# A row softmax on one core: five of eight tile loads move from Sync's queue to ScalarE's, ahead of the stores

## Chip, cores and metric

The kernel runs on one core of one Trainium2 chip. The metric is device time in microseconds (us) of one execution. It reads 33.55 MB from HBM and writes as much, so both the moving of data and the work on it matter.

## What is computed

A softmax over the last axis of a 16 x 1024 x 512 array of float32, with the input divided by a temperature of 0.5:

```python
def reference(x):
    temp = 0.5
    x_scaled = x / temp
    x_max = np.max(x_scaled, axis=-1, keepdims=True)
    exp_x = np.exp(x_scaled - x_max)
    return (exp_x / np.sum(exp_x, axis=-1, keepdims=True)).astype(np.float32)
```

## The kernel before

The 16,384 rows of 512 numbers are cut into eight tiles (`C = 8`, called chunks in the code). A tile holds 128 partitions with 16 rows each: 128 x 16 x 512 float32, 4.19 MB, 32 KB in each partition. There are six buffers (`BUFS`, L42), so tiles 6 and 7 reuse those of tiles 0 and 1. The order of the instructions is written out by hand (`manual_schedule`, L47): each engine and each queue works through its own instructions in program order, and the framework puts in the waits that the data needs.

Tile 0 is loaded in two pieces of 4 and 12 rows, all others whole (`LOADS`, L38). The work is done in 11 blocks (`BLOCKS`, L39): three for tile 0 (4, 4 and 8 rows), one for each of tiles 1 to 6, two of 8 rows for tile 7. Each tile is stored whole (`STORES`, L40), after its last block.

For a block, these steps follow one another:

- `load` (L59): the load of the block's tile, issued on Sync's queue (L66), if the tile has not been asked for yet. For tiles 6 and 7 the load has to wait until the store of tile 0 or 1 has landed, since it overwrites that buffer.
- `shift` (L68): VectorE takes the negated maximum of each row (L74) and doubles it (L78).
- `exponentials` (L80): ScalarE computes exp(2x - 2max) row by row, with the row's sum as a second result (L85).
- `scale_vector` (L95): VectorE takes the reciprocal of the sums (L100) and multiplies seven eighths of the rows (L102). `scale_scalar` (L106) leaves the last eighth to ScalarE (L111).
- `store` (L115): if the block ends its tile, ScalarE issues the tile's store on its own queue (L119).

The loop at the end (L123 to L133) staggers them: the exponentials of block i + 1 come before the scaling of block i, and the maximum of block i + 2 after it. On VectorE the order is thus scale i, maximum i + 2, scale i + 1, and so on.

Two hardware queues for transfers are in use. Sync's holds all loads: nine transfers, of which seven (tile 0's two pieces and tiles 1 to 5) are issued one after another at the start, as nothing holds them. ScalarE's holds the eight stores, from the moment that each tile is finished. Both queues are served by the same 16 transfer engines.

Before the first block, ScalarE loads its table of the exponential and runs it once on a dummy, `warm` (L50 to L52), so that the table is there when the first tile is.

Of the kernel before, what the change touches and what calls it, by code (L numbers as in the profile page):

```python
# [1 line left out]

# [4 lines left out]


@with_exitstack
def kernel(  # L10
    ctx: ExitStack,
    tc: tile.TileContext,
    x: bass.AP,
    out: bass.AP,
):
    nc = tc.nc
    fp32 = mybir.dt.float32
    P = nc.NUM_PARTITIONS
    AX = mybir.AxisListType.X
    EXP = mybir.ActivationFunctionType.Exp  # L20
    COPY = mybir.ActivationFunctionType.Copy
    MAX = mybir.AluOpType.max

    D = x.shape[-1]
    xf = x.flatten_outer_dims()
    of = out.flatten_outer_dims()
    N = xf.shape[0]

    G = 16
    C = N // (P * G)
    assert C * P * G == N
    xr = xf.rearrange("(c p g) d -> c p g d", p=P, g=G)
    outr = of.rearrange("(c p g) d -> c p g d", p=P, g=G)
    WHOLE = [(0, G)]
    LOADS = [[(0, 4), (4, G)]] + [WHOLE] * 7  # L38
    BLOCKS = [[(0, 4), (4, 8), (8, G)]] + [WHOLE] * 6 + [[(0, 8), (8, G)]]  # L39
    STORES = [WHOLE] * 8  # L40
    BMAX = 16
    BUFS = 6  # L42

    data = ctx.enter_context(tc.tile_pool(name="data", bufs=BUFS))
    stats = ctx.enter_context(tc.tile_pool(name="stats", bufs=6))

    ctx.enter_context(tc.manual_schedule())  # L47


    warm = stats.tile([P, 1], fp32, name="warm", bufs=1)  # L50
    nc.vector.memset(warm, 0.0)  # L51
    nc.scalar.activation(out=warm, in_=warm, func=EXP)  # L52

    chunks = {}
    blocks = [(c, lo, hi) for c in range(C) for lo, hi in BLOCKS[c]]
    n = len(blocks)
    biases, sums, recips = {}, {}, {}

    def load(c):  # L59
        if c < BUFS:  # L60
            chunks[c] = data.tile([P, G, D], fp32, name="xt")
        else:
            chunks[c] = chunks[c - BUFS]
        xt = chunks[c]
        for lo, hi in LOADS[c]:
            nc.sync.dma_start(out=xt[:, lo:hi, :], in_=xr[c][:, lo:hi, :])  # L66

    def shift(i):  # L68
        c, lo, hi = blocks[i]
        if c not in chunks:  # L70
            load(c)
        b = hi - lo
        negmax = stats.tile([P, BMAX], fp32, name="negmax")
        nc.vector.tensor_reduce(  # L74
            negmax[:, 0:b], chunks[c][:, lo:hi, :], axis=AX, op=MAX, negate=True
        )
        biases[i] = stats.tile([P, BMAX], fp32, name="bias")
        nc.vector.tensor_scalar_mul(biases[i][:, 0:b], negmax[:, 0:b], 2.0)  # L78

    def exponentials(i):  # L80
        c, lo, hi = blocks[i]
        sums[i] = stats.tile([P, BMAX], fp32, name="sums")
        for g in range(hi - lo):
            row = chunks[c][:, lo + g, :]
            nc.scalar.activation(  # L85
                out=row,
                in_=row,
                func=EXP,
                bias=biases[i][:, g : g + 1],
                scale=2.0,  # L90
                accum_out=sums[i][:, g : g + 1],
            )


    def scale_vector(i):  # L95
        c, lo, hi = blocks[i]
        b = hi - lo
        k = b - b // 8
        recips[i] = stats.tile([P, BMAX], fp32, name="recip")
        nc.vector.reciprocal(recips[i][:, 0:b], sums[i][:, 0:b])  # L100
        rows = chunks[c][:, lo : lo + k, :]
        nc.vector.tensor_mul(  # L102
            rows, rows, recips[i][:, 0:k].unsqueeze(2).broadcast_to((P, k, D))
        )

    def scale_scalar(i):  # L106
        c, lo, hi = blocks[i]
        b = hi - lo
        for g in range(b - b // 8, b):
            row = chunks[c][:, lo + g, :]  # L110
            nc.scalar.activation(  # L111
                out=row, in_=row, func=COPY, scale=recips[i][:, g : g + 1]
            )

    def store(i):  # L115
        c, _, end = blocks[i]
        for lo, hi in STORES[c]:
            if hi == end:
                nc.scalar.dma_start(  # L119
                    out=outr[c][:, lo:hi, :], in_=chunks[c][:, lo:hi, :]  # L120
                )

    shift(0)  # L123
    shift(1)
    exponentials(0)
    for i in range(n):
        if i + 1 < n:
            exponentials(i + 1)
        scale_vector(i)
        scale_scalar(i)  # L130
        if i + 2 < n:
            shift(i + 2)
        store(i)  # L133


# [1 line left out]
_INS = ['x']  # L137
_OUTS = [((16, 1024, 512), 'float32')]


# [23 lines left out]
```

## Time and profile before

| | us |
|---|---|
| median of 6 runs | 162.36 (162.09 to 162.48) |
| profiled execution, its time | 162.26 |
| profiled execution, its span | 160.5 |
| VectorE (DVE) busy | 134.6 (84%) |
| ScalarE (ACT) busy | 102.1 (64%) |
| VectorE idle, waiting for loads | 9.6 |
| first store issued | 45.67 |
| last store issued | 147.64 |

The span runs from the first to the last instruction that the profiler saw; the rest of the execution's time, 1.76 us, lies around it. In the lines of the profile, L66 is line 66 of the kernel, DVE is VectorE, ACT is ScalarE, SP is Sync, and ACTq and SPq are the parts of ScalarE and Sync that issue transfers. A group's row gives its line, engine and operation, output and input, shapes and count, then the busy time, the mean in ns of one, and the idle time before it with what ended it. These are the largest groups:

```profile
L85 ACT ACTIVATE xt<-xt,bias 128x512 f32<-128x512 f32 x128 | 90.4, 708 | 41.8 <-DVE bias L78 41.3
...
L102 DVE TENSOR_TENSOR xt<-xt,recip 128x7168 f32<-128x7168 f32 (+2 forms) x11 | 62.0, 5637 | 0.4
```

The section on transfers counts the issues and gives the size of each in KB and the median time from issue to landing:

```profile
out_dram<-xt ACTq DMA_DIRECT2D x8, 4096.0 KB, 22.8
xt<-in_x_dram SPq DMA_DIRECT2D x7, 4096.0 KB, 30.3
xt<-in_x_dram SPq DMA_DIRECT2D x1, 3072.0 KB, 11.8
xt<-in_x_dram SPq DMA_DIRECT2D x1, 1024.0 KB, 5.0
```

The single transfers, as the trace has them:

| transfer | issued at | us to landing |
|---|---|---|
| tile 0, first piece | 0.73 | 5.0 |
| tile 0, second piece | 1.15 | 11.8 |
| tile 1, 2, 3 | 1.63, 2.09, 2.80 | 21.0, 30.3, 39.5 |
| tile 4, 5 | 3.29, 3.78 | 52.9, 71.7 |
| tile 6, 7 | 69.64, 89.00 | 25.3, 26.0 |
| store 0, 1 | 45.67, 59.12 | 23.9, 29.8 |
| store 2, 3 | 75.74, 92.36 | 32.6, 28.6 |
| store 4, 5 | 108.98, 125.59 | 21.7, 14.7 |
| store 6, 7 | 133.17, 147.64 | 16.8, 12.0 |

### The profile page before, as it was taken

To read this page: it belongs to the slowest core of one execution; us is meant where nothing else is said; L and a number is where in the kernel's file an instruction comes from. 1 tells how busy PE (TensorE), PEld (TensorE's weight loads), DVE (VectorE), ACT (ScalarE), POOL (GpSimd) and SP (SyncE) were. 2 spreads that over 40 slices of the span, in tenths; PEclk is the share of its full clock that TensorE was granted. 3 is DMA by queue.
4 is the path that set the end of the run, shared out by engine and by line. 5 is a ranking of instruction groups with operands and counts; after the bars stand their busy time and mean duration, and the time that the engine had idled before them with its cause. 6 is when DMAs were issued, how large, how long until landed. Compare 5 with 4: busy or idle time off the path is not lost.

```text
span 160.5 us, 402 instructions
## 1 busy us (share of the span) xinstructions
DVE 134.6 (84%) x45; ACT 102.1 (64%) x273; POOL 0.2 (0%) x4
## 2 busy tenths in 40 slices
DVE  0507999999999999999999999999999999957000
ACT  3071549069979972998199909991899891690000
POOL 0000000000000000000000000000000000000000
DMA  5999999999999999999999999999999999999993
GB/s 180 468 431 482 400 400 490 417 392 459 449 400 376 408 408 490 408 400 498 408 392 498 417 392 484 417 400 466 441 400 433 474 400 417 490 400 400 498 408 139
DMA packets 2450, 67.13 MB, mean 418 GB/s; under 512 B 272, under 2 KB 272, under 8 KB 272
## 3 DMA queue, kind: packets, MB, share of 16 engines
q1 hardware_dynamic: 1296, 33.56, 49.3%
q10 hardware_dynamic: 1152, 33.55, 48.4%
q14 instruction: 2, 0.02, 0.0%
HBM read 33.55 MB, written 33.55 MB: 418 GB/s over the span
## 4 chain that ended last, share of the span: by engine, by line
DVE 80%; DMA 7%; ACT 4%; issue 0%; SPq 0%
DVE negmax L74 42%; DVE xt L102 36%; DMA xt<-in_x_dram 7%; ACT xt L85 4%; DVE bias L78 1%; DVE recip L100 1%; SPq L66 0%
## 5 line engine op out<-in xcount | busy, mean ns | idle before, releaser
L85 ACT ACTIVATE xt<-xt,bias 128x512 f32<-128x512 f32 x128 | 90.4, 708 | 41.8 <-DVE bias L78 41.3
L74 DVE TENSOR_REDUCE negmax<-xt 128x16 f32<-128x8192 f32 (+2 forms) x11 | 69.9, 6352 | 9.6 <-DMA xt<-in_x_dram 9.6
L102 DVE TENSOR_TENSOR xt<-xt,recip 128x7168 f32<-128x7168 f32 (+2 forms) x11 | 62.0, 5637 | 0.4
L85 ACT ACTIVATION_READ_ACCUMULATOR xt<-xt,bias 128x1 f32 x128 | 23.9, 187 | 0.0
L111 ACT ACTIVATE xt<-xt,recip 128x512 f32<-128x512 f32 x15 | 9.9, 707 | 0.0
L100 DVE RECIPROCAL recip<-sums 128x16 f32<-128x16 f32 (+2 forms) x11 | 2.4, 218 | 1.8 <-ACT xt L85 1.8
L78 DVE TENSOR_SCALAR bias<-negmax 128x16 f32<-128x16 f32 (+2 forms) x11 | 1.9, 173 | 0.4
L52 ACT ACT_TABLE_LOAD x1 | 1.3, 1283 | 0.7 <-PEq L148 0.7
L51 DVE MEMSET warm<- 128x1 f32 x1 | 0.1, 59 | 0.8 <-PEq L148 0.8
L52 ACT ACTIVATE warm<-warm 128x1 f32<-128x1 f32 x1 | 0.2, 203 | 0.0
L148 POOL MEMSET const-bfloat16-1.0<- 128x1 bf16 x1 | 0.1, 102 | 0.0
L148 POOL MEMSET const-uint8-127<- 128x1 uint8 x1 | 0.1, 102 | 0.0
L148 POOL MEMSET const-float32-0.0<- 128x1 f32 x1 | 0.1, 99 | 0.2 <-issue 0.2
L148 POOL MEMSET const-float32-1.0<- 128x1 f32 x1 | 0.1, 99 | 0.0
## 6 DMA issues: line engine op xcount, KB each, us to landing
out_dram<-xt ACTq DMA_DIRECT2D x8, 4096.0 KB, 22.8
xt<-in_x_dram SPq DMA_DIRECT2D x7, 4096.0 KB, 30.3
xt<-in_x_dram SPq DMA_DIRECT2D x1, 3072.0 KB, 11.8
xt<-in_x_dram SPq DMA_DIRECT2D x1, 1024.0 KB, 5.0
```

Of the source, the lines that this page charges most:

```text
L51: nc.vector.memset(warm, 0.0)
L52: nc.scalar.activation(out=warm, in_=warm, func=EXP)
L74: nc.vector.tensor_reduce(negmax[:, 0:b], chunks[c][:, lo:hi, :], axis=AX, op=MAX, negate=True)
L78: nc.vector.tensor_scalar_mul(biases[i][:, 0:b], negmax[:, 0:b], 2.0)
L85: nc.scalar.activation(out=row, in_=row, func=EXP, bias=biases[i][:, g : g + 1], scale=2.0, accum_out=sums[i][:, g : g + 1],)
L100: nc.vector.reciprocal(recips[i][:, 0:b], sums[i][:, 0:b])
L102: nc.vector.tensor_mul(rows, rows, recips[i][:, 0:k].unsqueeze(2).broadcast_to((P, k, D)))
L111: nc.scalar.activation(out=row, in_=row, func=COPY, scale=recips[i][:, g : g + 1])
L148: nc = _bacc.Bacc("TRN2", target_bir_lowering=False, num_devices=1)
```

## The change

The loads of tiles 0 to 4 (`FIRST = 5`) are issued on ScalarE's queue, all of them before anything else of the kernel, so that they stand ahead of the stores in that queue. Sync's queue keeps the loads of tiles 5, 6 and 7. A dependency is added by hand: the load of tile 5 waits until that of tile 4 has landed. The dummy exponential with its table load moves behind the five tiles' loads in program order. Nothing else changes: tile sizes, buffers, blocks, stores and arithmetic stay.

```diff
+    FIRST = 5
+    first_loads = []
...
-
-
-    warm = stats.tile([P, 1], fp32, name="warm", bufs=1)
-    nc.vector.memset(warm, 0.0)
-    nc.scalar.activation(out=warm, in_=warm, func=EXP)
...
         for lo, hi in LOADS[c]:
-            nc.sync.dma_start(out=xt[:, lo:hi, :], in_=xr[c][:, lo:hi, :])
+            queue = nc.scalar if c < FIRST else nc.sync
+            last = queue.dma_start(out=xt[:, lo:hi, :], in_=xr[c][:, lo:hi, :])
+
+        if c == FIRST - 1:
+            first_loads.append(last.ins.name)
+        if c == FIRST:
+            tc.add_manual_dep(
+                last.ins,
+                first_loads[0],
+                mybir.DependencyInfo(
+                    mybir.DependencyClass.Sync, mybir.DependencyReason.DATA
+                ),
+                reason="one queue of loads at a time",
+            )
...
+    for c in range(FIRST):
+        load(c)
+
+
+    warm = stats.tile([P, 1], fp32, name="warm", bufs=1)
+    nc.vector.memset(warm, 0.0)
+    nc.scalar.activation(out=warm, in_=warm, func=EXP)
+
     shift(0)
     shift(1)
     exponentials(0)
```

## The prediction

> **What bounds the kernel now.** I read the slices of the span first, then the moved bytes over longer windows, then the landing of each transfer, then the chain of work and the queue's waits. The slices come from the page:
>
> ```profile
> DMA  5999999999999999999999999999999999999993
> ...
> HBM read 33.55 MB, written 33.55 MB: 418 GB/s over the span
> ```
>
> The transfer engines are at nine tenths or more in 38 of 40 slices, while the chain of work that ended last is mostly VectorE. Two limits lie close together here. The windows (columns: stretch, length, busy time of DVE, ACT, POOL, clock, DMA share, GB/s) say how close to its best the transfer side is:
>
> ```profile
> 20.00:45.00 25.00, 24.86 (x9) 17.11 (x49) 0.00 (x0) 1.00 1.01 434
> 45.00:50.00 5.00, 4.93 (x4) 4.17 (x12) 0.00 (x0) 1.00 0.98 347
> 50.00:55.00 5.00, 5.00 (x2) 5.00 (x17) 0.00 (x0) 1.00 0.97 419
> 55.00:80.00 25.00, 24.86 (x8) 16.99 (x46) 0.00 (x0) 1.00 1.01 438
> 80.00:105.00 25.00, 24.93 (x6) 20.99 (x59) 0.00 (x0) 1.00 0.99 428
> 105.00:130.00 25.00, 24.86 (x8) 20.52 (x55) 0.00 (x0) 1.00 1.01 434
> ```
>
> Loads alone (20 to 45 us), loads and stores mixed (55 to 105) and mostly stores (105 to 130) all run at 428 to 438 GB/s. So the mix of directions costs nothing in itself, and total bytes set the time. One place differs: 45 to 50 us at 347 GB/s. The first store is issued at 45.67, so this dip is the moment at which stores join a running stream of loads. No later join shows one.
>
> The landing times agree. Adding to each issue's start its time to landing, stores 3 to 7 land at 121.0, 130.7, 140.3, 150.0 and 159.6: a step of 38.6 / 4 = 9.66 us, and 4.194 MB / 9.66 us is 434 GB/s. Store 7 is issued at 147.64, 2.3 us before store 6 lands, and takes 12.0 us. It therefore had no free run: it came behind store 6. The chain shows what holds the issue of store 7:
>
> ```profile
> 137.65 5.76 ACT xt L85 x16
> 143.41 0.02 issue
> 143.44 0.21 DVE recip L100
> 143.65 0.02 issue
> 143.67 3.89 DVE xt L102
> ```
>
> VectorE runs from 12.97, the landing of the second piece of tile 0, almost without a gap until 137.6, and the last block's work ends at 147.56. So a change that delays the first tile, or any transfer at all, appears at the end in full; a change that hastens only the transfers can gain no more than store 7's small wait.
>
> **The change, part by part.** All is summed against the profiled execution: 162.26 us, with a span of 160.5 and 1.76 around it. The median of the runs is 162.36, 0.10 above, and I shift by that at the end.
>
> (a) Six load issues (tile 0 in two pieces, tiles 1 to 4) go from Sync to ScalarE. ScalarE's first instruction starts at 0.72, Sync's first load at 0.73, so the first byte comes at the same time: 0. On Sync the seven early issues lasted 0.37 to 0.67 us and were over at 4.3; ScalarE's own issues last 0.34 to 0.37. Six take 2.1 us (ScalarE's rows) to 3.1 (3.57 / 7 x 6, Sync's). I take 2.6; ScalarE is through at 3.3.
>
> (b) The table load (1.28) and the warming exponential (0.20) now follow: done at 4.8, at most 5.4. ScalarE's first real work starts at 8.23 and waited 6.01 us for it, so 2.8 us of idle time remain: cost 0. Without that cover the first four exponentials (8.23 to 11.17) still had 4.2 us until VectorE takes their sums at 15.37. VectorE's memset, 0.06 us, moves within its wait for tile 0: 0.
>
> (c) Stores now stand behind tiles 0 to 4 in one queue. Tile 3 lands at 42.3; with no store in between, tile 4 lands 9.7 later, at 52.0 (before 56.2). Store 0, issued at 45.67, cannot share from the start as it did; it follows tile 4, and as it has been issued 6 us earlier there is no gap at the handover.
>
> (d) Sync waits for tile 4 before it issues tile 5: 52.0 in place of 3.78. Behind that wait stand only the loads of tiles 6 and 7. From issue to first byte Sync's first load needed about 1.1 us (37 GB/s x 2 us = 0.07 MB in the first 2 us, which is 0.17 us of full rate). Nothing would move for that time if Sync's were the only queue with work; store 0 fills it. Cost 0; without store 0 it would be 1.1 to 2.6 (1 MB landed in 5.0 us and needs 2.4).
>
> (e) Then follow the queues at 9.66 us a tile, halved while both have work. Store 0 runs alone for about 2 us, shares the rest (7.7 x 2) and lands near 69.3, with a dip near 70.3 (before 69.6). Tile 5 lands near 74 (before 75.5; VectorE wants it at 87.4). Tile 6 waits for store 0, comes in behind tile 5 and lands near 94 (wanted at 104.0). Tile 7 waits for store 1 (near 90) and lands near 113 (wanted at 120.65). Slack is 13, 10 and 7.6 us, so VectorE's row does not move. Stores 2 to 7 have all been issued by the time that the queue reaches them (75.7, 92.4, 109.0, 125.6, 133.2 against 90, 109, 121, 130, 140), and there is no moment without queued work. The same bytes at the same rate end at the same time.
>
> (f) The dip is left. Its price: (433 - 347) x 5 / 433 = 1.0 us from the five-microsecond window; (433 - 383) x 10 / 433 = 1.15 from the ten after 45; and from the landings, twelve tiles after 42.3 at 9.66 each should end at 158.3, the last landed at 159.6, which is 1.3. I take 1.0. Before, it came where a second queue, with stores, joined loads. After, the second queue joins too, once, near 53 us, but with loads into stores. No row shows that join. Bounds: it costs nothing and the 1.0 is gained, or each of the two new transitions (stores after loads in one queue, loads joining stores) costs 1.0 and 1.0 is lost. The nearest row is a join of a second queue, once; I take the same 1.0, a difference of 0.
>
> The Trainium skill's DMA: Bandwidth & Descriptors (Issuing engines are not separate DMA queues; Queues, rings and completion order) says that transfers from all engines share the same 16 engines, which take turns between queues packet by packet, and that spreading issues saves only issue time. That speaks against any effect at all, and would price a join at nothing; the row of 347 GB/s disagrees with it at this one spot. By the rule the sum is 0, by the row it is 0 as well, but only because one join takes the place of another. The same page (Anatomy of one DMA) gives each transfer some 2 us of fixed cost, most of it waiting for the receipt, which speaks against waiting for a landing before the next issue; by it step (d) without cover would cost 2.0, and no run here shows it alone.
>
> Sum: 162.26 + 0 = 162.26, on the runs' median 162.36; I say 162.4.
>
> **The rivals.** *No dip.* If stores that follow loads in the same queue start without a stall and loads join stores without one, transfers are 1.0 us early from 53 on; store 6 lands at 149.0 and store 7 may land at 158.6, 11.0 after its issue. For: the rate later, with both queues working, is undisturbed. Against: the nearest row of a 4 MB transfer without a queue ahead, tile 0, took 12.2 (0.73 to 12.95), by which store 7 gains nothing; but its first 4 us ran below the rate (37, then 324 GB/s). Between -1.0 and 0; I take -0.8: 161.6.
>
> *A dearer join.* The place is 50 to 56 us. If the stores' start behind tile 4 costs its 1.0 as before, and the loads' join costs as much again, the queues run 1.0 late from there. Since they are never empty, nothing gives it back: 163.4. It decides from the first tenth that the join loses beyond 1.0, as store 7 already waits for store 6. For: the first load of the kernel also ran slowly at its start. Against: tiles 6 and 7 entered beside stores at 69.64 and 89.00 with no loss, though behind a load in their own queue.
>
> *It does not do what it says.* If the table load still stands first on ScalarE, the first load is issued 1.28 late, and both VectorE's row and the transfers end 1.28 late: 163.6. For: the table load is ScalarE's first instruction now. Against: it belongs to the warming exponential, which the diff moves.
>
> **How the numbers follow.** One dip as before 0.45, no dip 0.28, a dearer join 0.23, table load first 0.04. The likeliest gives 162.4; its own range is 162.1 to 162.75, the spread of the three prices of the dip. A measurement of this kernel tells about 0.2% (0.32 us) from no change. Of the first case 0.36 falls within that, 0.04 below and 0.05 above; of the second 0.26 is faster and 0.02 not to be told; the others are slower. Faster 0.30, within 0.2% 0.38, slower 0.32. The range takes in both neighbours' middles and leaves out their far ends and the table load: 161.5 to 163.4.
>
> **What would show it.** Step (a): ScalarE's first issue near 0.72 and the first piece landed near 5.7, the second near 12.95. (c): tile 4 landed near 52, no store before it. (d): Sync's first issue near 52. (e): VectorE's idle time by loads unchanged at 9.6 us, last store issued near 147.6. (f): windows between 45 and 60 us, one of them below 400 GB/s for some 5 us; none says "no dip", two or a deeper one says "dearer". The forecast is wrong if store 7 takes over 12.8 or under 11.4 us, or if its issue moves.

## The result and the profile after

The changed kernel takes 163.17 us (median of 16 runs, 162.75 to 163.64), against 162.32 for the kernel before (35 runs). The ratio is 1.005, with a 95% interval of 1.0041 to 1.0059: slower by half a per cent, or 0.85 us. The profiled execution took 163.09 us with a span of 161.2, 0.7 more than before.

First the start of the kernel, in the timeline of the changed kernel (start, duration, engine, line, operation, and in brackets the idle time before it with what ended it):

```profile
0.72 3.14 ACTq L65 DMA_DIRECT2D xt<-in_x_dram  x6
...
3.90 1.28 ACT L140 ACT_TABLE_LOAD   x1 [3.90 <-issue]
5.19 0.20 ACT L140 ACTIVATE warm<-warm 128x1 f32<-128x1 f32 x1
...
8.00 0.72 ACT L96 ACTIVATE xt<-xt,bias 128x512 f32<-128x512 f32 x1 [2.61 <-DVE bias L89]
```

The six loads are issued from 0.72 on, and the table load follows them. ScalarE still sits idle for 2.6 us before its first real work, so neither costs anything. The first piece of tile 0 lands at 5.45, against 5.7 in the kernel before.

The waits of Sync's queue (who waited for whom: us in all, times, longest) and the chain's end:

```profile
SPq L65 <- DMA xt<-in_x_dram: 52.5, 1, 52.5
SPq L65 <- DMA out_dram<-xt: 34.2, 2, 18.9
```

```profile
137.43 5.76 ACT xt L96 x16
143.19 0.02 issue
143.21 0.21 DVE recip L111
143.43 0.02 issue
143.45 3.89 DVE xt L113
```

Sync does wait 52.5 us for tile 4 and issues tile 5 at 53.22. VectorE's work ends 0.2 us earlier than before (143.45 against 143.67 for the last multiplication), so the lost time is not on any engine. The last store is issued at 147.43 and needs 12.9 us in place of 12.0: it stands longer behind store 6. The trace on this store (duration of the issue in ns, its start, and the time to landing):

```profile
L130 ACTq DMA_DIRECT2D out_dram<-xt x1: 338/338/338, 147.4 to 147.4; - x1
...
DMA to landing us min/median/max: 12.9/12.9/12.9
```

Where the transfers lost it shows in the windows of the changed kernel (stretch, length, DVE, ACT, POOL, clock, DMA share, GB/s):

```profile
20.00:45.00 25.00, 24.86 (x9) 17.33 (x49) 0.00 (x0) 1.00 1.02 438
45.00:50.00 5.00, 4.93 (x4) 4.16 (x12) 0.00 (x0) 1.00 0.97 360
50.00:55.00 5.00, 5.00 (x2) 5.00 (x15) 0.00 (x0) 1.00 1.00 380
55.00:80.00 25.00, 24.86 (x8) 16.98 (x45) 0.00 (x0) 1.00 1.00 430
80.00:105.00 25.00, 24.93 (x6) 20.99 (x59) 0.00 (x0) 1.00 1.00 430
105.00:130.00 25.00, 24.86 (x8) 20.52 (x56) 0.00 (x0) 1.00 1.02 440
```

There is one dip, as before, and it is larger. From 433 GB/s, 45 to 50 loses (433 - 360) x 5 / 433 = 0.84 us and 50 to 55 loses 0.61: 1.45 in all, against 0.99 + 0.16 = 1.15 by the same two windows before. It is over when tile 4 has landed, at 53.2. The load of tile 5, which joins the stores after that, costs nothing: the windows from 55 on scatter as they did before.

The windows give a mean over 16 transfer engines; the end is set by the slowest of them. Counted by landings, as the prediction did: tile 3 lands at 42.2, twelve tiles at 9.66 should end at 158.1, the last lands at 160.3. That is 2.2 us lost, against 1.4 before (the prediction's 1.3 has 158.3 where 42.3 + 115.9 is 158.2). So beyond the mean dip, the slowest engine has lost about 0.7 us after the change and 0.2 before.

To put a finer number on both, I use the records of the single transfers. One of 32 KB lasts 1.213 us in the undisturbed stretches of every run here. The "dip" below is what the transfers between 44 and 64 us lasted beyond that (or beyond the share of it that a smaller one takes), added up and divided by 16; the "lag" is the end of the last engine's work minus the mean of the 16 ends. Before: dip 0.87, lag 0.82. After: dip 1.26, lag 1.21. The two differences of 0.39 make 0.78, of which 0.1 is given back by the earlier start; the span grew by 0.7. Both figures come from one execution of each kernel, whose time is up to 0.4 us away from the median of its runs.

The same records show which transfers are slow, and it is not the stores. Before, 27 transfers between 44 and 64 us lasted noticeably longer, 1.27 to 2.11 us each: all are loads on Sync's queue that start between 47.05 and 49.13, and the first transfer of store 0 starts at 49.78. After, there are 31, of 1.33 to 2.33 us: all stand on ScalarE's queue and start between 48.27 and 50.57, and as no engine has finished tile 4 before 51.8, they are loads too. So in both kernels the time is lost by the loads that run just ahead of the first store's data.

### The profile page after: what moved, and what is told of

It is laid out like the page before. It is cut to its first block, busy times and chain, and to the rows that moved or that the text cites. A ratio compares the mean times of both kernels' runs of the same rounds, so it can differ in the third digit from the quotient of the medians.

```text
span 161.2 us, 402 instructions
## 1 busy us (share of the span) xinstructions
DVE 134.6 (84%) x45; ACT 102.1 (63%) x273; POOL 0.2 (0%) x4
## 4 chain that ended last, share of the span: by engine, by line
DVE 80%; DMA 7%; ACT 4%; issue 0%; ACTq 0%
DVE negmax L85 42%; DVE xt L113 36%; DMA xt<-in_x_dram 7%; ACT xt L96 4%; DVE bias L89 1%; DVE recip L111 1%; ACTq L65 0%
```

## The experiments

Each kernel is compared with the kernel before on the same chip, over five rounds. Where an edit starts from the changed kernel, the diff is against that.

**The wait without the move** (wait_only): `queue = nc.sync` for all loads, with the five early loads no longer ahead of the dummy exponential; only the dependency of tile 5 on tile 4 stays.

```diff
-            queue = nc.scalar if c < FIRST else nc.sync
+            queue = nc.sync
...
-    for c in range(FIRST):
-        load(c)
```

> All loads on Sync's queue as before, and tile 5 waits until tile 4 has landed: the wait without the move. Theory Q (the dip, 0.9 us before and 1.3 us after the change, is deeper because the first store follows a load in the same queue): the dip stays at about 0.9 us near 47 to 51, the time at 162.3. Theory L (it is deeper because no load runs on beside the first store): loads stop when tile 4 has landed, near 56, and start again near 58; another 0.4 us is lost, 162.7 to 163.2. Theory J (loads joining stores cost): a loss of about 1 us near 58 to 60, 163.3.

Measured: 162.66 us against 162.30, ratio 1.0021 (1.0009 to 1.0032). Dip 0.85 as in the kernel before, lag 0.95, and no loss where tile 5 joins the stores near 58 to 60:

```profile
45.00:55.00 10.00, 9.93 (x5) 9.17 (x26) 0.00 (x0) 1.00 0.96 380
55.00:65.00 10.00, 9.93 (x4) 6.00 (x16) 0.00 (x0) 1.00 1.00 429
```

In this execution the wait does not deepen the dip, and theories L and J have no support. But the profiled execution, 162.37, is the quickest of the twelve, and the median lies 0.36 above the kernel before, more than Q expected. Tile 7 now lands at 119.8, less than a microsecond before VectorE takes it up; the loss on the median may come from there, which was not tried.

**The move without the wait** (queue_only): tiles 0 to 5 on ScalarE's queue.

```diff
-    FIRST = 5
+    FIRST = 6
```

> Tiles 0 to 5 all on ScalarE's queue, tiles 6 and 7 on Sync's: the move without the added wait (tile 6 has to wait for store 0 anyway). The first store then follows tile 5, near 62. Q and L: a dip of about 1.3 us near 57 to 62, and 163.1 as after the change. J: as the join of tile 6 with the stores near 71 also costs, 163.1 or more, with a loss near 72 to 75. If the added wait is what costs, 162.3.

Measured: 163.22, ratio 1.0053 (1.0038 to 1.0069), the same loss as the whole change. The windows of this run show one dip, now where store 0 follows tile 5, and none after it, when tile 6 joins at 72:

```profile
45.00:57.00 12.00, 11.93 (x5) 11.17 (x32) 0.00 (x0) 1.00 0.97 418
57.00:63.00 6.00, 5.96 (x3) 2.00 (x6) 0.00 (x0) 1.00 1.02 366
63.00:75.00 12.00, 11.97 (x3) 12.00 (x34) 0.00 (x0) 1.00 1.00 431
```

Dip 1.08, lag 1.13. So the move alone brings the whole loss, without the added wait.

**Store 0 alone on Sync's queue** (store0_sync).

```diff
-                nc.scalar.dma_start(
+                (nc.sync if c == 0 else nc.scalar).dma_start(
```

> As after the change, but store 0 alone is issued on Sync's queue, ahead of the load of tile 5, so it joins tile 4 from another queue. Q: a dip of about 0.9 us near 47 to 51 and 162.3 to 162.5. L: no load is queued behind tile 4 before 62, so the dip is 1.3 us and the time 163.1. J: tile 5 joins store 1 near 62, 163.1 or more with a loss there.

Measured: 162.75 over twelve runs that reach from 162.21 to 166.76; ratio 1.0023 (1.0001 to 1.0045) without the four longest, of 164.89 and more. The dip is 0.96, between those of the kernel before and the changed one. The six quickest runs (162.21 to 162.47) are as quick as the kernel before, which no run of the changed kernel is. The others are another matter. In the one that was profiled, of 163.03, tile 5 stands behind store 0, and tile 7 lands so late that VectorE waits for it:

```profile
121.78 4.42 DVE L85 TENSOR_REDUCE negmax<-xt 128x8 f32<-128x4096 f32 x1 [1.03 <-DMA xt<-in_x_dram]
```

This speaks for Q by the quickest runs; the dip and the median leave its price open.

**Tile 5 beside tile 4** (early5): the dependency is on tile 3.

```diff
-        if c == FIRST - 1:
+        if c == FIRST - 2:
```

> As after the change, but tile 5 waits for tile 3 in place of tile 4, so that it runs beside tile 4 from about 44, and is still running when store 0 follows tile 4 near 59. Q: store 0 still follows a load in its own queue, a dip of 1.3 us near 56 to 60, 163.1. L: a load runs on beside the first store, a dip of 0.9 and 162.3 to 162.5. J: no load joins stores before the one of tile 6, which comes while tile 5's queue is already empty, 163.1.

Measured: 163.29, ratio 1.0062 (1.005 to 1.0075); dip 1.09, lag 1.60. The dip has moved with store 0, to 53 to 60 us:

```profile
53.00:60.00 7.00, 7.00 (x2) 6.12 (x16) 0.00 (x0) 1.00 1.00 365
```

A load runs on in the other queue and the loss stays, which is against L. Store 0 still follows a load in its own queue. Yet of the 26 slow transfers 25 belong to tile 5 in Sync's queue, not to tile 4 ahead of the store: the other queue's loads pay too.

**The queues exchanged** (swap): from the kernel before, all loads on ScalarE's queue, all stores on Sync's; the dummy exponential follows the early loads, as in the change.

```diff
-            nc.sync.dma_start(out=xt[:, lo:hi, :], in_=xr[c][:, lo:hi, :])
+            nc.scalar.dma_start(out=xt[:, lo:hi, :], in_=xr[c][:, lo:hi, :])
...
-                nc.scalar.dma_start(
+                nc.sync.dma_start(
...
+    for c in range(BUFS):
+        load(c)
...
+        if i == 4 or i == 5:
+            load(i + 2)
```

> The kernel before with its queues exchanged: all loads on ScalarE's queue (tiles 6 and 7 issued after the stores of blocks 4 and 5 in program order, near 76 and 92 us), all stores on Sync's. Theory Q (the first store costs more where it follows a load in its own queue): it joins from another queue, a dip of 0.9 us, 162.3. Theory I (loads through ScalarE's queue cost by themselves, whatever the stores do): 163.1.

Measured: 162.22, ratio 0.9999 (0.9985 to 1.0013); dip 0.68, lag 0.82. Loads through ScalarE's queue cost nothing by themselves. The profile has a second, unexplained slow spot of 0.6 us near 87, so the profiled execution is not one of the quickest.

**Store 0 in two pieces** (small_before from the kernel before, small_after from the changed one): the first transfers of the store are 8 KB for a partition.

```diff
-                nc.scalar.dma_start(
-                    out=outr[c][:, lo:hi, :], in_=chunks[c][:, lo:hi, :]
-                )
+                for a, b in [(0, 4), (4, G)] if c == 0 else [(lo, hi)]:
+                    nc.scalar.dma_start(
+                        out=outr[c][:, a:b, :], in_=chunks[c][:, a:b, :]
+                    )
```

> The kernel before, with store 0 issued as two transfers of 4 and 12 rows, one right after the other, so that the first transfers of stores are 8 KB for a partition in place of 32. If the dip is a fixed time or a fixed number of bytes: 0.9 us as before, 162.3. If it is a share of one transfer of one partition: 0.2 to 0.3 us, and a time of 161.6 to 161.8, as the last store then waits less.

> The same split of store 0 in the changed kernel. Fixed time or bytes: a dip of 1.3 us, 163.1. A share of one transfer: 0.3 to 0.4 us, 162.2 to 162.3.

Measured: 162.30, ratio 1.0008 (0.9988 to 1.0027), dip 0.68, lag 0.74; and 163.69, ratio 1.0076 (1.0055 to 1.0097), dip 1.02, lag 1.77. Neither came down to the 0.2 to 0.4 of a share of one transfer, so the dip is not set by the size of the first transfers. The premise did not hold quite: the first piece was issued at 41.3, not beside the second at 45.6, because ScalarE's issues run ahead of its arithmetic.

**Four tiles in place of five** (first4).

```diff
-    FIRST = 5
+    FIRST = 4
```

> The changed kernel with four tiles on ScalarE's queue in place of five: tile 4 waits on Sync until tile 3 has landed at 42.2, when no store has been issued, so nothing covers the wait; and store 0 joins tile 4 from another queue. Q: an uncovered wait of 1.1 to 2.6 us at 42 to 45 and a dip of 0.9, so 163.4 to 164.9, with transfers standing still before 45.

Measured: 165.07, ratio 1.017 (1.0148 to 1.0192), above the 163.4 to 164.9 that were expected. The windows show the uncovered wait:

```profile
40.00:41.00 1.00, 1.00 (x1) 1.00 (x3) 0.00 (x0) 1.00 0.84 360
41.00:42.00 1.00, 1.00 (x1) 1.00 (x5) 0.00 (x0) 1.00 0.01 0
42.00:43.00 1.00, 1.00 (x1) 1.00 (x4) 0.00 (x0) 1.00 0.00 0
43.00:44.00 1.00, 1.00 (x1) 1.00 (x4) 0.00 (x0) 1.00 1.93 524
```

Tile 3's last transfers start before 41 and it has landed at 42.2; tile 4 is issued at once, and its first transfers start after 43. The window from 35 to 45 has 312 GB/s, (433 - 312) x 10 / 433 = 2.8 us, and the median grew by 2.8. In the single transfers this falls into two parts: the 16 engines end tile 3 at 41.3 and start tile 4 at 43.4 on the mean, a standstill of 2.1 us, and the first transfers of tile 4 last 1.4 to 2.3 us in place of 1.213, which costs 0.7 more. Store 0 then joins tile 4 from another queue with a dip of 0.81.

**The first store held back** (late0): on the kernel with tile 5 beside tile 4, store 0 is issued together with store 1 in program order.

```diff
-        store(i)
+        if i == 3:
+            store(2)
+        if i != 2:
+            store(i)
```

> As with tile 5 beside tile 4 (tile 5 waits for tile 3), and store 0 is held back and issued together with store 1, near 59, when tile 4 has just been read, so that no load stands ahead of it in ScalarE's queue any more; tile 5 still runs on Sync's. Theory Q (it is the load ahead in its own queue that deepens the first store's dip): a dip of 0.9 us near 60 to 63, 162.3 to 162.6, unless the transfers run dry between tile 5 and the store, which would show as a gap. If loads on ScalarE's queue earlier in the run are enough to deepen it: 1.1 to 1.3 and 163.2.

Measured: 162.77, ratio 1.0020 (1.0008 to 1.0032); dip 0.87, lag 1.79. The store was issued at 54.1, not near 59, again ahead of the arithmetic, so tile 4 (landed at 59.4) still stood before it in the queue:

```profile
54.02 0.71 ACT L96 ACTIVATE xt<-xt,bias 128x512 f32<-128x512 f32 x1
54.14 0.35 ACTq L130 DMA_DIRECT2D out_dram<-xt  x1
...
56.84 0.70 ACT L96 ACTIVATE xt<-xt,bias 128x512 f32<-128x512 f32 x1
```

The premise fell, but the run still bears on Q. A load stood ahead of store 0 in its own queue, as in the changed kernel, and the dip was 0.87, not the 1.1 to 1.3 of that case; the time lies between the two groups, and the profiled execution (163.16) has lost its time in the lag.

**A second turn from loads to stores** (second_turn): tile 5 goes behind store 0 on ScalarE's queue, ahead of store 1; the dependency moves to tile 6.

```diff
-            queue = nc.scalar if c < FIRST else nc.sync
+            queue = nc.scalar if c <= FIRST else nc.sync
...
-        if c == FIRST:
+        if c == FIRST + 1:
...
         store(i)
+        if i == 2:
+            load(FIRST)
```

> The changed kernel, with tile 5 also on ScalarE's queue, behind store 0, so that this queue turns from loads to stores a second time (tile 5, then store 1, near 72 to 82). If each such turn costs: a second dip of about 1.1 to 1.3 us between 65 and 85 and 164.2 to 164.5. If only the first store of the run costs, for instance since it is the first write to the output: no second dip, 163.1.

Measured: 163.39, ratio 1.0067 (1.0053 to 1.0080). The windows:

```profile
45.00:50.00 5.00, 4.93 (x4) 4.03 (x12) 0.00 (x0) 1.00 0.99 367
50.00:55.00 5.00, 5.00 (x2) 5.00 (x15) 0.00 (x0) 1.00 0.96 374
55.00:75.00 20.00, 19.93 (x5) 16.13 (x44) 0.00 (x0) 1.00 0.99 428
75.00:80.00 5.00, 4.93 (x4) 0.99 (x2) 0.00 (x0) 1.00 1.00 419
80.00:100.00 20.00, 19.93 (x5) 15.99 (x45) 0.00 (x0) 1.00 1.01 436
```

The first dip is that of the changed kernel. Near 78, where store 1 follows tile 5 in the same queue, the single transfers lose 0.14 us, not 1.2. So not each such turn pays as the first one does. That it is only the first store of a run that pays does not follow: tile 6 was running beside the second turn, which the first one did not have.

**An early first store** (first_write_after and first_write_before): rows 0 to 3 of tile 0 are stored as soon as they are scaled, near 18 us, on Sync's queue in the changed kernel and on ScalarE's in the kernel before; the rest of tile 0 follows as it did.

```diff
+        if i == 0:
+            nc.sync.dma_start(out=outr[0][:, 0:4, :], in_=chunks[0][:, 0:4, :])
         for lo, hi in STORES[c]:
             if hi == end:
+                lo = 4 if c == 0 else lo
```

> The changed kernel with rows 0 to 3 of tile 0 stored early, on Sync's queue as soon as they are scaled (near 18 us), and rows 4 to 15 later in ScalarE's queue behind tile 4 as before. If the dip belongs to the first store of the run: it comes near 18 to 22, with 0.9 us or less, and none is left at 48 to 53; 162.3 to 162.6. If it belongs to a queue's turn from loads to stores: 1.1 to 1.3 us again at 48 to 53, 163.1 or more.

> The kernel before with the same early store of four rows, on ScalarE's queue near 18 us, and the rest of tile 0 at 45.6. First store of the run: a dip near 18 to 22 alone, 162.0 to 162.4. Each coming of stores to loads alone: one dip near 20 and another of 0.9 near 48 to 51, 162.8 to 163.2.

Measured on the changed kernel: 162.88 against 162.40, ratio 1.0022 (1.0009 to 1.0036). Its windows:

```profile
15.00:30.00 15.00, 14.86 (x9) 8.68 (x24) 0.00 (x0) 1.00 0.96 402
...
45.00:50.00 5.00, 4.93 (x4) 4.17 (x12) 0.00 (x0) 1.00 0.97 419
50.00:55.00 5.00, 5.00 (x2) 5.00 (x16) 0.00 (x0) 1.00 1.07 452
```

The dip behind tile 4 is gone: 0.11 us between 44 and 64, and 0.46 at 19 to 22, where the early store joins. About half of the change's loss is recovered, with the queues and the wait as the change has them; 0.48 us remain on the median, more than was expected, and the lag is still 1.34. Some 0.4 us are lost near 65 to 67 in the profiled execution, for which I have no cause.

Measured on the kernel before: 162.11 against 162.40, ratio 0.9975 (0.9963 to 0.9986), with all runs between 161.98 and 162.22. This beats both kernels. The dip did not shrink as a whole (0.46 at 19 to 22 and 0.47 near 50, 0.93 in all against 0.87); the lag is 0.53 in place of 0.82, so what it gains lies at the slowest engine. That rests on one profile each. The store near 46, not the first of the run here, still costs half of what it cost, which neither expectation had.

The readings side by side, sorted by how the first store meets the loads; "profiled" is the time of the execution that dip and lag are from:

| kernel | median, us | ratio | profiled | dip | lag |
|---|---|---|---|---|---|
| from another queue: before | 162.32 | 1 | 162.26 | 0.87 | 0.82 |
| queues exchanged | 162.22 | 0.9999 | 162.66 | 0.68 | 0.82 |
| before, store 0 in two pieces | 162.30 | 1.0008 | 162.09 | 0.68 | 0.74 |
| wait without the move | 162.66 | 1.0021 | 162.37 | 0.85 | 0.95 |
| store 0 alone on Sync's queue | 162.75 | 1.0023 | 163.03 | 0.96 | 0.57 |
| four tiles in place of five | 165.07 | 1.017 | 165.28 | 0.81 | 1.11 |
| behind a load in its own queue: after | 163.17 | 1.005 | 163.09 | 1.26 | 1.21 |
| move without the wait | 163.22 | 1.0053 | 163.02 | 1.08 | 1.13 |
| tile 5 beside tile 4 | 163.29 | 1.0062 | 163.60 | 1.09 | 1.60 |
| first store held back | 162.77 | 1.0020 | 163.16 | 0.87 | 1.79 |
| second turn | 163.39 | 1.0067 | 163.42 | 1.22 | 1.29 |
| after, store 0 in two pieces | 163.69 | 1.0076 | 163.77 | 1.02 | 1.77 |
| small store earlier, then behind a load | 162.88 | 1.0022 | 163.04 | 0.46 + 0.11 | 1.34 |
| small store earlier, then from another queue | 162.11 | 0.9975 | 162.12 | 0.46 + 0.47 | 0.53 |

The dip follows the way in which the first store comes, with one exception, the store held back. The lag follows something else. It is 1.1 to 1.8 us in eight of the nine kernels in which one queue holds loads and then stores, whatever the dip is, and 0.5 to 0.95 in the five in which each queue holds only one kind. (The ninth is store 0 alone on Sync's queue, whose last store was issued a microsecond late.) So about half of the change's loss, the 0.39 of the lag, may belong to the mixed queue and not to the first store. That fits the two kernels with a mixed queue and a dip no larger than before, the store held back and the small store earlier: each still loses 0.5 us on the median. But no run takes the lag away and leaves the dip, so this is not shown.

## Why the prediction was right, and where it was not

The time lies within the stated range of 161.5 to 163.4, but 0.8 us above the 162.4 of the likeliest case. No change within 0.2% had the highest chance, 0.38; the kernel became slower by 0.5%, which had 0.32. The range reaches the measured time only because it was drawn to take in the price of a rival, 163.4, and that rival's mechanism did not happen. In that the prediction was lucky.

- **What bounds the kernel** held. Transfers never pause between 5 and 158 us, what is lost near 50 is not made up later, and the early end of VectorE's work gained nothing.
- **Step (a)**: the six issues took 3.14 us and began at 0.72. That is just over the upper bound, which the profile's 3.53 us for Sync's seven issues would put at 3.0 (the prediction has 3.57 and 3.1). Right in that it cost nothing.
- **Step (b)**: the table load ended before ScalarE was wanted, with 2.6 us left of the 2.8 that were worked out. The rival of a table load ahead of the loads is out.
- **Steps (c) and (e)**: tile 4 landed at 53.2, not 52.0, since the dip fell on it; tiles 5, 6 and 7 landed at 77.0, 96.4 and 115.8, two to three microseconds after the estimates and well before VectorE asked. The last store's issue came 0.2 us earlier, with VectorE's earlier start. Right in what mattered.
- **Step (d)**: the wait cost nothing, as store 0 covered it; the price without cover is 2.8 us by first4, above the 1.1 to 2.6 that were given. The landing of one load, the issue of the next and its first byte make up the standstill of 2.1 us; the 0.7 of slow first transfers came on top, and my upper bound did not allow for both. The Trainium skill's page DMA: Bandwidth & Descriptors (Anatomy of one DMA) gives about 2.0 us of fixed cost for a transfer. It fits that figure on transfers issued from GpSimd, and these are issued from ScalarE and Sync; the standstill of 2.1 is near it, and the 0.7 is not in it.
- **Step (f)** is the step that failed, and it failed in what it took to be the same. It let one dip, at the joining of a second queue, take the place of another at the same price. The second queue's joining, tile 5 into stores, costs nothing. The dip stays with the first store of the run, and in its new place behind a load in its own queue it is larger: 1.26 us by the single transfers in place of 0.87 (1.45 by the windows in place of 1.15). The lag of the slowest engine, for which the sum had no term, grew by as much, from 0.82 to 1.21. The term of the sum was 0 and measured 0.85.
- **The rival "a dearer join"** gave 163.4, near the time, and about the right place: 50 to 56 us, where the slow transfers run from 48.3 to 52.9. Its argument that nothing gives the loss back was right. Its mechanism, two dips of which the second is the loads' join, is refuted by the windows after 55. By its own signs the likeliest case was wrong: a last store of over 12.8 us would refute it, and it took 12.9; two windows below 400 GB/s (360 and 380) spoke for the dearer join.
- **The rule that spreading issues over several engines saves only issue time** (the same page, Issuing engines are not separate DMA queues) agrees with the runs in which queue carries the loads (swap, 0.9999). It says nothing of what the order within a queue costs, which is 0.85 us here.

What stays open: why loads slow down ahead of the first store, why more so when it stands in the queue of the loads, and why the last of the 16 engines then lags further. The runs show where and how much; they do not show what an engine does in that time.

## What to carry to other kernels

Where transfers never pause, look in windows of a few microseconds for the stretches that fall below the steady rate, and price a reordering by what it does to those; the steady rate itself did not care which queue a load came from. Try letting the first store reach the engines from a queue that has no loads standing before it, and starting it early and small if a small one is ready; that was the quickest kernel here. A wait for a landing before the next load is free only while another queue has work.

## What the runs showed of the hardware that was not expected

- The first coming of stores costs most, and the loads pay it: the 27 slow transfers of the kernel before and the 31 of the changed one are all loads, of up to 2.3 us in place of 1.213. A second turn from loads to stores in one queue lost 0.14 us where the first had lost 1.2, and after a small early store the turn behind tile 4 lost 0.11; from another queue, though, the store after the early one still lost 0.47.
- ScalarE's issues of transfers run ahead of the arithmetic before them in program order: in late0, store 0 was issued at 54.14, while the exponentials that precede it in the program went on until 57.5.
- A load that waits for another's landing leaves the engines without a new transfer from before 41 to after 43 us, and costs 2.8 us of full rate with nothing else queued: 2.1 of standstill and 0.7 of slow first transfers.
